# Order of squares, token sums and weight sums around the second norm of a hybrid encoder block

## The chip, the core and the metric

The kernel runs on one core of one Trainium2 chip. The time is device microseconds of one execution; of several runs the median is given. Beside the times there is one profiled execution, whose trace holds every instruction of every engine: TensorE (PE, with its weight loads as PEld), VectorE (DVE), ScalarE (ACT), GpSimd (POOL) and the DMA queues of SyncE (SP), ScalarE and GpSimd.

## The reference

One encoder block over 1024 tokens of width 1024, all in float32. Only the second half of it is touched by the change.

```python
h = rms_norm(x, norm1_g)
proj = h @ w_in                        # q, k, v (8 heads x 64) and u
a = neighbourhood_attention(q, k, v, rpb)
p = multiscale_pool(u, w_pool, pool_scale)
x = x + concat(a, p) @ w_out
h2 = rms_norm(x, norm2_g)              # x * rsqrt(mean(x*x) + 1e-6) * g
x = x + (silu(h2 @ w_gate) * (h2 @ w_up)) @ w_down     # d_ff = 2816
```

## The kernel before

**Number format.** Every operand of a product is split into a high part (a cast to fp32r on ScalarE) and a residue (a subtraction on VectorE), by the helper `split`; the helpers `cook_w` and `split_op` call it for weights and activations. A product is three matmuls: high x high, high x low, low x high. TensorE writes to PSUM banks of 128x512.

**Stages.** Projections and attention come first, up to about 314 us. Then the output product is finished: the residual stream lies transposed in eight tiles `x2[0..7]` of [128, 2, 512], where `x2[0..3]` are the first half of the tokens and `x2[4..7]` the second. Each half tile needs eight blocks `c` of the mixed channels (three matmuls each). For the first half, six of the blocks have been multiplied ahead; `w_full(t, nh, (2, 3), 1)` adds the last pair of blocks, 2 and 3, of which block 3 needs the attention's last values. For the half tiles `t` = 4 and 5 of `nh` = 0, six blocks stand open in PSUM: their generators lie in the list `tail`, and each `next` issues one more block. The other half tiles are done whole (24 matmuls). VectorE adds each finished bank into `x2` (line 818).

**The second norm.** For each token half: ScalarE squares the tiles (`square`, line 948), GpSimd adds the squares into one (line 950), `fold` adds the two halves of that tile on GpSimd (line 956) and splits it, and `tok_sum` lets TensorE sum over the channels with a matrix of ones into the bank `ss`. The last tile of the second half, `x2[7]`, is not added on GpSimd but squared and split in two parts (`square1`, line 960), so the second half has three pairs of token sums. `scale2` makes the reciprocal root (VectorE 968, ScalarE 972 and 973, VectorE 974 to 976), `norm2` scales `x2` in place (VectorE, 984). `store` writes the un-normalised tiles to DRAM through ScalarE's queue.

**Gate and up products.** They are computed from 2x2 block operands with seven products instead of eight, by sums of weights and of activations. A unit `i` is one of 22 (gate and up of 11 column groups). Of each weight, `sum_w` makes the sums s1, s2, s3 (GpSimd, lines 1023 to 1025; for unit 3 VectorE) and `sum_4` the sum s4, in place of block "12" (GpSimd, line 1015), which must wait for the split of "12" and of s2. Activations get sums t1 to t4 (`sub`, line 998). A unit's products are `first` (block 11), `second` (12), `part_y` (s2 x t2), `part_z` (s3 x t3), `part_w` (s1 x t1), `part_4` (22 x t4) and `part_5` (s4 x 22); `add` (line 1063) combines their banks on VectorE, `settle` applies silu (ScalarE, 1068) or multiplies gate and up (line 1072). Units 0 to 3 are interleaved by hand in the order written out below line 1149; from unit 4 on a loop runs, where `sum_4` is called in `cook_w(i, "s4")`. `park` combines a finished pair of units (GpSimd, 1133) and stores it to DRAM with four DMAs from GpSimd's queue (lines 1139 to 1142). The down product reads these tiles back at the end, from about 800 us.

**What sets the order.** Each engine runs its instructions in one fixed order. A scheduler sets that order when the kernel is built, from a model of the times and the order of the program. Instructions passed through `keep` (ScalarE), `keepd` (VectorE), `keepp` (GpSimd) or the matmul helper `mm` keep the order of the program among themselves while the flag `pin_act`, `pin_dve`, `pin_pool` or `pin` is true; all others may be moved. `pin` and `pin_pool` are true from the pairs of blocks 2 and 3 on, `pin_act` and `pin_dve` from just behind `w_full(7, 1)`, all four to just before the loop. Tiles of SBUF come from a ring of 45 buffers of 4 KB a partition (`slot`), so a load can also wait for a buffer to be freed. Loads of weights (`fetch_w`, line 1008) go through SyncE's queue.

Of the kernel before, what the change touches and what calls it, by code (L numbers as in the profile page):

```python
# [42 lines left out]
EARLY = 4  # L43
# [6 lines left out]
def hybrid_block(ctx, tc, xT, xt, w1, wu, rpbx, wpool, wout, wgu, wd, sm, out):  # L50
    nc = tc.nc
# [50 lines left out]
    def keep(i):  # L102
        if pin_act:
            tc.keep_in_program_order(i)
# [5 lines left out]
    def keepp(i):  # L110
        if pin_pool:
            tc.keep_in_program_order(i)
# [374 lines left out]
    pin_act = pin_dve = True  # L487
    for i in range(4):
# [3 lines left out]
        else:  # L492
            g = cook_w1_(0, 0)
# [8 lines left out]
    pin_act = pin_dve = False  # L502
# [17 lines left out]
    pin_act = pin_dve = True  # L520
# [306 lines left out]
    x2 = []  # L827
# [94 lines left out]
    def act_op(o):  # L922
        ACTO[o] = [
            [slot(F32R, f"b{o}_{q}_{nm}", [P, 2, 512]) for nm in "hl"] for q in range(2)
        ]
# [8 lines left out]
    def tok_sum(hf, hl, first, last):  # L934

        if first:
            ps2[hf] = bank(pop, f"ss_{hf}")
        for n in range(2):
            mm(ps2[hf], ones, hl[:, n], start=first and n == 0, stop=last and n == 1)

    def store(hf, q):
        nc.scalar.dma_start(out=x2d[q + 4 * hf], in_=x2[q + 4 * hf])

    acc = {}

    def square(hf, q):
        s = slot(F32, f"sq_{hf}_{q}", [P, 2, 512])
        keep(nc.scalar.activation(s, x2[q + 4 * hf], AF.Square))
        if q:
            keepp(nc.gpsimd.tensor_tensor(out=acc[hf], in0=acc[hf], in1=s, op=ALU.add))  # L950
        else:
            acc[hf] = s
# [10 lines left out]
    def scale2(hf):  # L963
        n = slot(F32, f"n2_{hf}", [P, 2, 512])
        n2[hf] = y = slot(F32, f"y2_{hf}", [P, 512])
        v, a = n[:, 0], n[:, 1]
        keepd(
            nc.vector.tensor_scalar(
                out=v, in0=ps2[hf], scalar1=1.0 / DM, scalar2=EPS, op0=ALU.mult, op1=ALU.add
            )  # L970
        )
        keep(nc.scalar.activation(a, v, AF.Ln))
        keep(nc.scalar.activation(y, a, AF.Exp, scale=-0.5))
        keepd(nc.vector.tensor_tensor(out=a, in0=y, in1=y, op=ALU.mult))
        keepd(nc.vector.scalar_tensor_tensor(out=a, in0=a, scalar=-0.5, in1=v, op0=ALU.mult, op1=ALU.mult))
        keepd(nc.vector.scalar_tensor_tensor(out=y, in0=a, scalar=1.5, in1=y, op0=ALU.add, op1=ALU.mult))

    def norm2(hf, *qs):
        for q in qs:
            x = x2[q + 4 * hf]  # L980
            for i in range(2):
                k = 2 * q + i
                keepd(
                    nc.vector.scalar_tensor_tensor(
                        out=x[:, i],
                        in0=x[:, i],
                        scalar=g2_sb[:, k : k + 1],
                        in1=n2[hf],
                        op0=ALU.mult,
                        op1=ALU.mult,  # L990
                    )
                )

    def split_op(o, q, src):
        split(*ACTO[o][q], src)

    def sub(out, a, b_):
        keepd(nc.vector.tensor_tensor(out=out, in0=a, in1=b_, op=ALU.subtract))
# [4 lines left out]
    def fetch_w(i):  # L1003
        m, f = MF[i]
        raww[i] = []
        for j in range(2):
            r = slot(F32, f"raw_{'gu'[m]}_{f}_{j}", [P, 2, 512])
            nc.sync.dma_start(out=r, in_=wgu[m, f, j])
            raww[i].append(r)
        (r0, r1) = raww[i]  # L1010
        sums[i] = {"11": r0[:, 0], "12": r1[:, 0], "22": r1[:, 1], "s3": r0[:, 1], "s4": r1[:, 0]}

    def sum_4(i):
        x = sums[i]["12"]
        keepp(nc.gpsimd.tensor_tensor(out=x, in0=x, in1=sums[i]["s2"], op=ALU.subtract))
# [12 lines left out]
    def cook_w(i, o):  # L1028
        if i < EARLY and o in ("11", "12"):
            w = rg.tile([P, 2, 512], F32R, tag="w", name=f"w_{i}_{o}")  # L1030
        else:
            w = slot(F32R, f"w_{i}_{o}", [P, 2, 512])
        wop[i, o] = w
        if o == "s4" and i >= EARLY:
            sum_4(i)
        split(w[:, 0], w[:, 1], sums[i][o])

# [46 lines left out]
    def part_y(i, y, hook=None):  # L1084
        u2 = res[i][0][:, 1]
        ps = bank(y, f"y_{i}")
        product(i, ps, "s2", "t2", False)
        if hook:
            hook("s2")
        add(u2, ps, u2)  # L1090
# [38 lines left out]
    def park(i):  # L1129
        f = MF[i][1]  # L1130
        a, b_ = res[i]
        sa, sb = res[i - 1]
        tt = lambda **k: keepp(nc.gpsimd.tensor_tensor(**k))  # L1133
        tt(out=sa[:, 0], in0=a[:, 1], in1=b_[:, 1], op=ALU.add)
        tt(out=sa[:, 1], in0=sa[:, 0], in1=a[:, 0], op=ALU.subtract)
        tt(out=sb[:, 0], in0=a[:, 0], in1=a[:, 1], op=ALU.subtract)
        tt(out=sb[:, 1], in0=b_[:, 0], in1=sa[:, 1], op=ALU.subtract)
        d = gsd[f].rearrange("o p n -> p o n")
        nc.gpsimd.dma_start(out=d[:, 0:1], in_=a[:, 0:1])
        nc.gpsimd.dma_start(out=d[:, 1:3], in_=b_)  # L1140
        nc.gpsimd.dma_start(out=d[:, 3:5], in_=sa)
        nc.gpsimd.dma_start(out=d[:, 5:7], in_=sb)
        del res[i], res[i - 1]

    def w_full(t, nh, cs=eight, n=2):
        for _ in w_out(t, nh, cs, n):
            pass

    pin = pin_pool = True
    for nh in range(2):  # L1150
        for t in range(4):
            w_full(t, nh, (2, 3), 1)
            if t % 2:
                store(0, 2 * nh + t // 2)
                square(0, 2 * nh + t // 2)
# [12 lines left out]
    square(1, 0)  # L1168
    w_full(6, 0)
    tok_sum(0, hl, True, True)  # L1170
    scale2(0)
    for q in range(4):
        norm2(0, q)
        split_op("11" if q < 2 else "21", q % 2, x2[q])
    w_full(7, 0)
    store(1, 1)
    square(1, 1)
    fetch_w(2)
    cook_w(2, "11")
    cook_w(2, "12")  # L1180
    sum_w(2)
    for i in range(2):
        sum_4(i)
    for t in (4, 5):
        w_full(t, 1)
    store(1, 2)
    square(1, 2)
    hl = [fold(1)]
    sum_4(2)
    s67 = slot(F32, "sq_1_3", [P, 2, 512])  # L1190
    w_full(6, 1)
    hl.append(square1(s67, 0))
    w_full(7, 1)
    pin_act = pin_dve = True
    hl.append(square1(s67, 1))
    store(1, 3)
    tok_sum(1, hl[0], True, False)
    tok_sum(1, hl[1], False, False)
    xs = [bank(stp, f"x_{i}") for i in range(EARLY)]
    first(0, xs[0])  # L1200
    tok_sum(1, hl[2], False, True)
    scale2(1)
    first(1, xs[1])
    fetch_w(3)
# [23 lines left out]
    settle(2, 0, 0, xs[2])  # L1228
    settle(3, 0, 0, xs[3])
    part_y(0, mmp)  # L1230
    act_op("t3")
    sub(x2[4], x2[6], x2[4])
    split_op("t3", 0, x2[4])
    sum_w(3, nc.vector, keepd)
    sum_4(3)
    cook_w(3, "s2")
    part_y(1, mmp)
    sub(x2[5], x2[7], x2[5])
    part_y(2, mmp)
    cook_w(0, "s3")  # L1240
# [43 lines left out]
    park(1)  # L1284
    part_4(2)
    cook_w(4, "12")
    cook_w(3, "s4")
    part_5(2)
    cook_w(4, "s2")
# [262 lines left out]
```

## Time and profile before

| | us |
|---|---|
| median of 3 runs (1018.28 to 1020.58) | 1018.47 |
| profiled execution | 1017.6 |
| its span, first to last instruction | 1015.2 |
| TensorE busy in the span | 992.9 (98%) |
| VectorE busy | 673.7 (66%) |
| ScalarE busy | 415.5 (41%) |
| GpSimd busy | 386.4 (38%) |

The granted TensorE clock is 0.993 of full speed on average. A busy TensorE is one with a matmul in flight, so its 98% includes matmuls that run at a lower clock. In a line of the timeline stand the start, the duration, engine, line of the kernel, operation, output and inputs by the program's names, and in square brackets how long the engine was idle before and what ended that. A line of the chain has start, duration and what. A duration on VectorE or GpSimd includes the time for which the instruction is held once it has begun.

### The profile page before, as it was taken

How to read it: one execution, taken by the hardware profiler on the slowest of the kernel's cores; microseconds unless marked ns; L12 is line 12 of the kernel's file. 1: busy time of each engine (PE TensorE's matmuls, PEld its weight loads, DVE VectorE, ACT ScalarE, POOL GpSimd, SP SyncE). 2: the span in 40 equal slices, each digit the busy share in tenths (PEclk: the TensorE clock that was granted, in tenths of full speed). 3: DMA queues.
4: the chain of work that ended last, by engine and by line, in shares of the span. 5: the costliest groups of instructions: out<-in, count | busy, mean ns of one | idle time of the engine just before them, and what ended most of it. 6: DMA issues, size and time to landing. Idle time of an engine off the chain costs nothing.

```text
span 1015.2 us, 13245 instructions
## 1 busy us (share of the span) xinstructions
PE 992.9 (98%) x4801; PEld 843.0 (83%) x4801; DVE 673.7 (66%) x1076; ACT 415.5 (41%) x796; POOL 386.4 (38%) x424
## 2 busy tenths in 40 slices
PE   9999999999999969998999999999999999999998
PEld 9988989998887857786888888888888888888887
DVE  5778777657843759876865555545561599988872
ACT  7634665656633433433333233233241354432500
POOL 0001433333422551068767757657743400000170
PEclk9999999999999979999999999999999999999999
DMA  9412642347814220124233323323317984373302
GB/s 357 177 57 87 220 135 65 100 134 261 267 42 146 84 83 21 53 93 145 76 121 114 110 88 114 103 94 114 110 57 229 357 287 142 101 235 122 125 32 94
DMA packets 56177, 135.88 MB, mean 134 GB/s; under 512 B 5872, under 2 KB 14832, under 8 KB 56112
## 3 DMA queue, kind: packets, MB, share of 16 engines
q1 hardware_dynamic: 48032, 106.45, 31.6%
q0 software_dynamic: 6784, 24.38, 6.3%
q10 hardware_dynamic: 1296, 4.21, 1.1%
q8 instruction: 38, 0.62, 0.3%
q14 instruction: 27, 0.22, 0.1%
HBM read 98.05 MB, written 32.77 MB: 129 GB/s over the span
## 4 chain that ended last, share of the span: by engine, by line
PE 85%; POOL 5%; DVE 5%; issue 2%; ACT 2%; DMA 0%; ACTq 0%; POOLq 0%; DVEq 0%
PE pj L85 12%; PE x L85 11%; PE w L85 10%; PE z L85 9%; PE pc L85 6%; PE pa L85 6%; PE pd L85 6%; PE pw L85 5%; PE y L85 5%; PE pu L85 4%; PE pb L85 3%; PE po L85 3%; PE s L85 2%; PE pt L90 2%; POOL gr L1133 1%
## 5 line engine op out<-in xcount | busy, mean ns | idle before, releaser
L85 PE MATMUL x<-b_h,w 128*128 128x512 f32 x352 | 115.8, 392 | 0.0
L85 PE MATMUL pw<-mx,wo 128*128 128x512 f32 x384 | 91.1, 392 | 1.4 <-ACT mx L763 0.8
L85 PE MATMUL pj<-w1h,xh 128*128 128x384 f32 x256 | 87.6, 347 | 1.7 <-DVE vnl L302 1.7
L85 PE MATMUL pj<-w1l,xh 128*128 128x384 f32 x256 | 84.8, 335 | 1.1 <-DVE w1l L116 1.1
L85 PEld LDWEIGHTS pw<-mx,wo 128*128 128x128 f32 x384 | 71.0, 188 | 16.7 <-ACT mx L763 1.2
L622 POOL TENSOR_SCALAR e<-e,r 64x128 f32<-64x128 f32 (+2 forms) x96 | 52.8, 564 | 83.1 <-DVE r L617 44.6
L85 PE MATMUL pj<-w1h,xl 128*128 128x384 f32 x256 | 83.8, 336 | 0.0
L1477 POOL TENSOR_TENSOR x2r<-x2r,u 128x512 f32<-128x512 f32 x12 | 23.8, 2018 | 149.8 <-DMA raw_a<-gsd 149.8
L1072 POOL TENSOR_TENSOR ur<-ur,gr 128x512 f32<-128x512 f32 x33 | 51.8, 1572 | 70.0 <-DVE ur L1063 31.4
L85 PEld LDWEIGHTS x<-b_h,w 128*128 128x128 f32 x352 | 66.8, 190 | 14.0
L85 PE MATMUL x<-b_l,w 128*128 128x512 f32 x176 | 68.9, 392 | 0.0
L85 PE MATMUL w<-b_h,w_s 128*128 128x512 f32 x176 | 59.1, 397 | 3.5 <-ACT w_s L115 3.1
L116 DVE TENSOR_TENSOR w_s<-sa,w_s 128x512 fp32r<-128x512 f32 x44 | 45.5, 1037 | 23.9 <-ACT w_s L115 23.8
L115 ACT CAST a_h<-raw_a 128x1024 fp32r<-128x1024 f32 (+1 forms) x42 | 41.0, 978 | 49.3 <-PE pc L85 13.8
L85 PE MATMUL y<-bt_h,w_s 128*128 128x512 f32 x176 | 57.7, 390 | 1.7 <-DVE w_s L116 0.9
L85 PE MATMUL z<-bt_h,w_s 128*128 128x512 f32 x176 | 57.9, 390 | 0.0
L85 PE MATMUL w<-bt_h,w_s 128*128 128x512 f32 x176 | 57.8, 389 | 0.0
L85 PE MATMUL z<-bt_h,w 128*128 128x512 f32 x176 | 57.8, 389 | 0.0
L116 DVE TENSOR_TENSOR a_l<-raw_a,a_h 128x1024 fp32r<-128x1024 f32 (+1 forms) x42 | 49.7, 1187 | 3.4 <-ACT a_h L115 3.1
L85 PEld LDWEIGHTS pj<-w1h,xh 128*128 128x128 f32 x256 | 48.5, 190 | 3.3 <-DVE vnl L302 2.5
L85 PEld LDWEIGHTS pj<-w1l,xh 128*128 128x128 f32 x256 | 48.1, 188 | 1.4 <-DVE w1l L116 1.4
L85 PEld LDWEIGHTS pj<-w1h,xl 128*128 128x128 f32 x256 | 48.1, 188 | 0.0
(267 smaller groups left out, 2646.5 us busy)
## 6 DMA issues: line engine op xcount, KB each, us to landing
raw_a<-gsd SPq DMA_DIRECT2D x77, 256.0 KB, 3.9
raw_g<-in_wgu SPq DMA_DIRECT2D x22, 512.0 KB, 3.8
raw_u<-in_wgu SPq DMA_DIRECT2D x22, 512.0 KB, 4.3
gsd<-gr POOLq DMA_DIRECT2D x22, 512.0 KB, 4.0
raw_d<-in_wd SPq DMA_DIRECT2D x20, 512.0 KB, 4.6
nb<-in_rpbx SPq DMA_DIRECT2D x24, 384.0 KB, 3.9
raw_w<-in_w SPq DMA_DIRECT2D x15, 384.0 KB, 4.5
gsd<-ur POOLq DMA_DIRECT2D x11, 512.0 KB, 3.3
```

The lines of the kernel that those rows point to most:

```text
L85: i = nc.tensor.matmul(*a, **k)
L90: i = nc.tensor.transpose(*a)
L115: keep(nc.scalar.copy(h, src))
L116: keepd(nc.vector.tensor_tensor(out=l, in0=src, in1=h.bitcast(F32), op=ALU.subtract))
L622: nc.gpsimd.tensor_scalar(out=out, in0=in0, scalar1=s1, scalar2=1.0, op0=ALU.mult, op1=ALU.mult)
L1072: k(eng.tensor_tensor(out=res[i][c][:, l], in0=src, in1=g, op=ALU.mult))
L1133: tt = lambda **k: keepp(nc.gpsimd.tensor_tensor(**k))
L1477: nc.gpsimd.tensor_tensor(out=q, in0=q, in1=U2[c], op=ALU.add)
```

## The change

Nothing is computed differently; instructions are put in another order, and more of them are held to it.

- `store` and the four DMAs of `park` are pinned as well.
- For the two open half tiles (`tail`), the block 2 product is issued ahead of the eight last pairs, block 3 behind them as before.
- `pin_act` is true from `scale2(0)` on instead of from behind `w_full(7, 1)`.
- `norm2` and `split_op` of the first half come behind `w_full(7, 0)`, `store(1, 1)`, `square(1, 1)` and `fetch_w(2)` instead of ahead of them.
- `sum_4(1)` moves from ahead of the `w_full(4, 1)` and `sum_4(2)` from ahead of `w_full(6, 1)`, both to behind the last `store`.
- `square(1, 2)` comes ahead of `store(1, 2)`.
- `first(0)` comes ahead of all token sums of the second half.
- `sum_w(3)`, `sum_4(3)` and the split of s2 of unit 3 come ahead of the sums t3.
- `sum_4(4)` is called behind `cook_w(4, "12")`, no longer in `cook_w(4, "s4")`, which stands behind `park(3)`.

```diff
     def store(hf, q):
-        nc.scalar.dma_start(out=x2d[q + 4 * hf], in_=x2[q + 4 * hf])
+        keep(nc.scalar.dma_start(out=x2d[q + 4 * hf], in_=x2[q + 4 * hf]))
...
-        if o == "s4" and i >= EARLY:
+        if o == "s4" and i > EARLY:
             sum_4(i)
...
-        nc.gpsimd.dma_start(out=d[:, 0:1], in_=a[:, 0:1])
-        nc.gpsimd.dma_start(out=d[:, 1:3], in_=b_)
-        nc.gpsimd.dma_start(out=d[:, 3:5], in_=sa)
-        nc.gpsimd.dma_start(out=d[:, 5:7], in_=sb)
+        keepp(nc.gpsimd.dma_start(out=d[:, 0:1], in_=a[:, 0:1]))
+        keepp(nc.gpsimd.dma_start(out=d[:, 1:3], in_=b_))
+        keepp(nc.gpsimd.dma_start(out=d[:, 3:5], in_=sa))
+        keepp(nc.gpsimd.dma_start(out=d[:, 5:7], in_=sb))
...
     pin = pin_pool = True
+    for g in tail:
+        next(g)
     for nh in range(2):
         for t in range(4):
             w_full(t, nh, (2, 3), 1)
...
     tok_sum(0, hl, True, True)
+    pin_act = True
     scale2(0)
-    for q in range(4):
-        norm2(0, q)
-        split_op("11" if q < 2 else "21", q % 2, x2[q])
     w_full(7, 0)
     store(1, 1)
     square(1, 1)
     fetch_w(2)
+    for q in range(4):
+        norm2(0, q)
+        split_op("11" if q < 2 else "21", q % 2, x2[q])
     cook_w(2, "11")
     cook_w(2, "12")
     sum_w(2)
-    for i in range(2):
-        sum_4(i)
+    sum_4(0)
     for t in (4, 5):
         w_full(t, 1)
+    square(1, 2)
     store(1, 2)
-    square(1, 2)
     hl = [fold(1)]
-    sum_4(2)
     s67 = slot(F32, "sq_1_3", [P, 2, 512])
     w_full(6, 1)
     hl.append(square1(s67, 0))
     w_full(7, 1)
-    pin_act = pin_dve = True
+    pin_dve = True
     hl.append(square1(s67, 1))
     store(1, 3)
-    tok_sum(1, hl[0], True, False)
-    tok_sum(1, hl[1], False, False)
+    for i in (1, 2):
+        sum_4(i)
     xs = [bank(stp, f"x_{i}") for i in range(EARLY)]
     first(0, xs[0])
-    tok_sum(1, hl[2], False, True)
+    for i in range(3):
+        tok_sum(1, hl[i], i == 0, i == 2)
     scale2(1)
     first(1, xs[1])
...
     part_y(0, mmp)
-    act_op("t3")
-    sub(x2[4], x2[6], x2[4])
-    split_op("t3", 0, x2[4])
     sum_w(3, nc.vector, keepd)
     sum_4(3)
     cook_w(3, "s2")
+    act_op("t3")
+    sub(x2[4], x2[6], x2[4])
     part_y(1, mmp)
+    split_op("t3", 0, x2[4])
...
     part_4(2)
     cook_w(4, "12")
+    sum_4(4)
     cook_w(3, "s4")
```

## The prediction

> **What bounds the kernel now.** I read the page first, its chain and slices.
>
> ```profile
> PE   9999999999999969998999999999999999999998
> PEclk9999999999999979999999999999999999999999
> ...
> PE 85%; POOL 5%; DVE 5%; issue 2%; ACT 2%; DMA 0%; ACTq 0%; POOLq 0%; DVEq 0%
> ```
>
> TensorE carries the chain; only slices 15 and 19 (355 to 381 us and 457 to 482 us) dip, so the change can gain only where TensorE waits. Next, busy time by stage (us; then busy us and records of PE, PEld, DVE, ACT, POOL; clock; DMA).
>
> ```profile
> 362.30:369.90 7.60, 0.00 (x0) 0.00 (x0) 1.56 (x2) 0.63 (x2) 7.52 (x6) 0.66 0.37 152
> 369.90:376.90 7.00, 6.63 (x19) 4.87 (x20) 2.48 (x3) 2.56 (x5) 0.56 (x1) 0.64 0.00 0
> 376.90:396.10 19.20, 19.20 (x86) 15.93 (x85) 16.96 (x22) 9.35 (x15) 0.62 (x1) 1.00 0.00 0
> 470.05:473.18 3.13, 0.00 (x0) 0.00 (x1) 0.71 (x2) 1.30 (x3) 3.11 (x4) 1.00 0.63 126
> 473.18:478.15 4.97, 4.56 (x13) 3.34 (x14) 4.97 (x4) 3.07 (x6) 3.83 (x3) 0.66 0.84 343
> 490.00:800.00 310.00, 310.00 (x1369) 256.72 (x1368) 169.24 (x206) 97.47 (x161) 188.52 (x148) 1.00 0.36 124
> ```
>
> The last row gives the free pace: 310 / 1369 = 0.227 us a matmul; from 490 us on nothing waits, so later stages only move along. Two stalls matter. **Stall B**: nothing runs from 362.3 to 369.9, then 18 matmuls (12 of `first(0)`, 6 token sums) run at a granted clock of 0.64 until 376.9. At the free pace they take 18 x 0.227 = 4.1 us; of 14.6 us, 10.5 are lost. **Stall D**: idle 3.13 us from 470.05, then 12 matmuls in 4.97 instead of 2.72 us: 5.4 us lost. Two small ones, A (315 us) and C (405 us), come below. The timeline and the chain say what ends B.
>
> ```profile
> 342.60 0.63 ACT L973 ACTIVATE y<-n 128x512 f32<-128x512 f32 x1
> 353.02 1.06 ACT L948 ACTIVATE sq<-x 128x1024 f32<-128x1024 f32 x1
> 354.15 2.40 POOL L950 TENSOR_TENSOR sq<-sq,sq 128x1024 f32<-128x1024 f32 x1 [12.30 <-ACT sq L948]
> 356.56 2.24 POOL sa L1023
> 358.87 2.15 POOL sa L1024
> ...
> 364.38 1.22 POOL raw_u L1015
> ...
> 367.97 1.27 POOL sq L956
> 369.27 0.63 ACT sq_hl_a L115
> 369.94 0.80 PE L85 MATMUL ss<-sq_hl_a,ones 128*128 128x512 f32 x1 [7.67 <-ACT sq_hl_a L115]
> ```
>
> GpSimd idles 12.3 us until `square(1,1)`, which stands on ScalarE behind four casts; then one add of squares, `sum_w(2)` (three), `sum_4(0)`, `sum_4(1)`, the next add of squares and the fold run one behind the other.
>
> **Part by part.**
>
> *Stall B.* `square(1,1)` moves ahead of norm2 and its casts: behind the Exp of `scale2(0)` (343.2) and a store issue (0.33), to 343.6 to 344.7, against 353.0 now. Its add on GpSimd starts near 345 instead of 354.15. `sum_4(1)` (1.22) and `sum_4(2)` leave the queue ahead of the fold. `first(0)` (12 matmuls, 2.7 us) goes ahead of all token sums, so TensorE has work from 362.3 to 365.0. Without a collision, the sums would end at 362.3 + 4.1 = 366.4: 10.5 us earlier. The store pinned behind the square delays nothing: norm2 of that tile stands some 20 us later.
>
> But the earlier GpSimd work now meets norm2 on VectorE, whose cover so far are GpSimd's 12.30 us of idleness.
>
> ```profile
> 346.60 5.38 DVE L984 SCALAR_TENSOR_TENSOR x<-x,sm_sb,y 128x512 f32<-128x512 f32 x8
> 353.03 1.21 DVE L116 TENSOR_TENSOR b_l<-x,b_h 128x1024 fp32r<-128x1024 f32 x1
> 354.17 0.68 DVE L818 TENSOR_TENSOR x<-pw,x 128x512 f32<-128x512 f32 x1
> 354.77 5.10 DVE L116 TENSOR_TENSOR b_l<-x,b_h 128x1024 fp32r<-128x1024 f32 x2
> 129.54 0.16 DVE L99 SCALAR_TENSOR_TENSOR rsq_q<-rsq_q,v 128x8 f32<-128x8 f32 x1
> 250.94 2.74 POOL L622 TENSOR_SCALAR e<-e,r 128x384 f32<-128x384 f32 x6 [6.82 <-DVE r L617]
> 252.14 1.22 DVE L99 SCALAR_TENSOR_TENSOR rsq_q<-rsq_q,v 128x8 f32<-128x8 f32 x1
> ```
>
> With GpSimd at work two `b_l` take 5.10 us where one alone took 1.21, and the sums 2.24 and 2.15 where the 128x512 fold took 1.27: they take turns. The add from PSUM stays at 0.68. Norm2 next to GpSimd is not in the trace. Its bounds: untouched (0.67 us each), or in full turns. The nearest row is L99, the same operation with two SBUF inputs: 0.16 us alone, 1.22 while GpSimd ran. I take turns.
>
> [...]
>
> In turns, from 345.4 (end of the `scale2` arithmetic, for which the load below waits): one add of squares 2.4 + four sums of 1.27 + eight norm2 of 0.67 = 12.9, to 358.3. Two `b_l` (2.4) and the add from PSUM that completes x2[6]: 361.3. `square(1,2)` 1.06, the add of squares 2.4, one `b_l` in between 1.2, the fold 1.27: 367.2. Cast 0.63, two half squares with their casts (four operations some 0.6 apart), the last VectorE residue 0.7, the last matmul: about **371.0**. If the last PSUM add stands behind two weight splits that alternate with `sum_4(1)` and `sum_4(2)`, 1.9 more. So `scale2(1)` and `first(1)` begin 376.9 - 371.0 = 5.9 us earlier; the seven products behind them run without a gap (19.2 us in the row to 396.1), so that shift carries on. TensorE has then idled most of 365 to 371, and after 3.13 us of idleness in stall D the clock fell to 0.66 and 12 matmuls lost 4.56 - 2.72 = 1.8. Today that slow stretch lies ahead of 376.9; then it lies behind. B brings 5.9 - 1.8 = **4.1**, ends 2 and 10.5.
>
> The loads decide too: `sum_w(2)` needs `fetch_w(2)`.
>
> ```profile
> 345.56 0.33 SPq L1008 DMA_DIRECT2D raw_g<-in_wgu  x1
> ...
> SPq L1008 <- DVE y L976: 4.5, 1, 4.5
> ...
> raw_g<-in_wgu SPq DMA_DIRECT2D x2, 512.0 KB, 3.5
> ```
>
> Its second half waits 4.5 us for a buffer that `scale2(0)` frees, then lands 3.5 us later, at 349: inside the 12.9 us counted, so nothing added.
>
> *Stall A, open products ahead.* Six matmuls (two products of block 2) move ahead of the eight last pairs.
>
> ```profile
> 315.42 0.50 PE L85 MATMUL pw<-mx,wo 128*128 128x512 f32 x1 [0.80 <-ACT mx L763]
> 316.15 1.21 PE L85 MATMUL pw<-mx,wo 128*128 128x512 f32 x4 [0.22 <-DVE mx L766]
> 333.24 1.12 DVE L116 TENSOR_TENSOR sq_hl_a<-sq,sq_hl_a 128x512 fp32r<-128x512 f32 x1 [3.33 <-ACT sq_hl_a L115]
> 334.46 0.62 PE L85 MATMUL ss<-sq_hl_a,ones 128*128 128x512 f32 x2
> ```
>
> They fill the 1.0 us wait, but the pairs still start at 316.15, so the first token sum is still ready at 334.36, just when TensorE arrives today (334.46). With six matmuls fewer between (1.4 us), TensorE now waits there. Late next: the fold. I take **0.2** (the first of the two sums goes early); ends -0.3 and 1.0.
>
> *Stall C, `sum_w(3)` ahead of t3.*
>
> ```profile
> 401.78 1.23 DVE L116 TENSOR_TENSOR bt_l<-x,bt_h 128x1024 fp32r<-128x1024 f32 x1 [1.12 <-ACT bt_h L115]
> ...
> 406.68 0.73 PE L85 MATMUL y<-bt_h,w_s 128*128 128x512 f32 x2 [0.91 <-DVE w_s L116]
> ...
> 414.22 0.19 PEld L85 LDWEIGHTS w<-bt_l,w_s 128*128 128x128 f32 x1 [0.52 <-DVE bt_l L116]
> ```
>
> The third part y waits for s2 of weight 3, now some 3 us earlier on VectorE: that wait goes. But the t3 splits move back behind it, and the first z needs them; VectorE's list up to the t1 split, for which the first w waits at 414.22, is the same in another order, and so is what is late next. Only a part of VectorE's 1.12 us of idleness can be won: **0.3**, ends -0.5 and 1.7 (0.8 + 0.9, both waits there).
>
> *Stall D, `sum_4(4)` earlier, GpSimd's stores pinned.*
>
> ```profile
> 456.87 0.73 POOL L1142 DMA_DIRECT2D gsd<-gr  x1
> 457.63 2.54 POOL L1072 TENSOR_TENSOR ur<-ur,gr 128x512 f32<-128x512 f32 x2
> 457.85 4.12 DVE L116 TENSOR_TENSOR w<-raw_g,w 128x512 fp32r<-128x512 f32 x1
> 471.20 1.27 POOL L1015 TENSOR_TENSOR raw_g<-raw_g,sa 128x512 f32<-128x512 f32 x1
> 472.51 0.62 ACT L115 CAST w_s<-raw_g 128x512 fp32r<-128x512 f32 x1 [1.07 <-POOL raw_g L1015]
> ```
>
> `sum_4(4)` runs at 471.20, behind the whole of `park(3)`; the cast at 472.51 and TensorE's s4 product wait for it. It moves behind `park(1)`, before the pair at 457.63. The pin also moves one store issue, which today runs in idle GpSimd time, into `park(1)` (0.73): start near 458.4 (457.63 and 0.73), end 459.7, cast 460.3, residue at the worst 4.1 (the row at 457.85): 464.4, where TensorE needs it at 470.05. The wait goes with 5 us to spare, and with it the slow clock: **5.4**, ends 3.1 (the idle alone) and 5.4. Behind it on GpSimd `sum_w(5)` and `park(3)` run some 2 us later; TensorE needs the former only after two more products (5.4 us), so nothing shows. The four issues of `park(3)`, one moved in as well, are read back only in the down stage.
>
> **The sum**, against the profiled execution (1017.6 us, span 1015.2; the median is 1018.47, 0.9 above): 4.1 + 0.2 + 0.3 + 5.4 = 10.0, so **1007.6 us**. By themselves the ends of B that I hold likely (sums 1.5 us earlier or later than 371.0) with C's and A's ends give 1005 to 1010.
>
> **The rivals.**
>
> *No turns: 1002.* Norm2 runs untouched next to GpSimd, or VectorE's list gets its PSUM adds early. Then norm2 ends at 352 as today, x2[6] is squared by 359, the sums end about 367.5, and TensorE hardly idles, so the clock stays: B = 9.4; 1017.6 - 9.4 - 5.4 - 0.5 = 1002.3. For it: the PSUM adds keep 0.68 next to GpSimd. Against: L99 and the `b_l` row. [...]
>
> *Stall D stays or its place is taken: 1012.* GpSimd runs without a gap from 457.6 to 475; with TensorE arriving 3 us earlier something else behind `sum_4(4)`, the i=5 sums first, may be late. Then D brings 0.5 to 2 of its 5.4: 1010 to 1013. Against: the 5 us to spare.
>
> *Nothing to measure: 1017.* The waits reappear in full: VectorE starts `scale2(1)` near 376, D stays. 1014.5 to 1020.7. Pinned order on three engines speaks against it.
>
> *Slower: 1024.* The buffer. `sq_1_1` is taken ten microseconds earlier, and buffers are short: the second load of `fetch_w(2)` waits 4.5 us already. If it must wait for one freed at the end of the output products (362.3) or later, `sum_w(2)`, pinned on GpSimd ahead of the squares, holds them up: load 3.5, three sums and `sum_4(0)` 5.1, squares 2.4, fold 1.3, cast and halves 3.6 give sums at 378.2 already. From a landing near 371.6 on, sums at 384, the loss (7.1, and 1.8 to the clock) outweighs A, C and D (5.9) by the 3 that can be measured. Landing at 375: 387.4, a loss of 12.3 - 5.9, about 1024. Against: the buffer freed by `scale2(0)` is freed as before, and loads now stand ahead of the `b` tiles in the program.
>
> **How the numbers follow.** About 0.3% (3.05 us) is what a measurement of this kernel can tell from no change. Forecast with turns (1005 to 1010) 0.50; no turns (1001 to 1005) 0.24; D not won (1010 to 1014) 0.13; nothing 0.08; slower 0.05. Faster: the first three, 0.87; same 0.08; slower 0.05. The range 1001.5 to 1013.5 takes in the first three but their edges, some 0.83. Its ends: 1001.5 is B without any collision (10.5), D in full and 0.2 of A and C; 1013.5 is B at 2, D at 2, the rest at nothing.
>
> **What would show it.** B: the second half's first add of squares on GpSimd near 345, norm2 rows stretched beyond 0.67 and the rows of `sum_w(2)` beyond 1.27; token sums after `first(0)`, the last near 371, a granted clock below 1 there. Norm2 at 5.4 in all and sums at 367 would show the first rival. A: no wait at 315, one of about 1 us before the first half's token sums. C: no wait in y, one in the first z. D: `sum_4(4)` near 458 in today's times, no idle ahead of the first s4 product there, clock 1.00. Wrong I am above all if VectorE's order of adds, which no pin fixes until 362, differs from today's, or if a load comes late.

## The result and the profile after

| | before | after |
|---|---|---|
| median of the comparison runs | 1018.38 us (4 runs) | 1009.33 us (4 runs) |
| lowest to highest | 1017.36 to 1020.58 | 1009.10 to 1009.74 |
| profiled execution, span | 1017.6, 1015.2 | 1009.33, 1007.0 |

The ratio after to before is 0.9909, with a 95% interval of 0.9892 to 0.9926: 9 us faster. The forecast was 1007.6 us with a range of 1001.5 to 1013.5.

The first view is the page of the changed kernel: the forty slices (25.2 us each) of TensorE and of its granted clock, and the chain's shares.

```profile
PE   9999999999999989999999999999999999999998
...
PEclk9999999999999989999999999999999999999999
...
PE 85%; DVE 6%; POOL 5%; issue 2%; ACT 1%; DMA 1%; DVEq 0%; POOLq 0%; ACTq 0%
```

The slice that held stall D (457 to 482 us) is at 9 tenths like its neighbours; the one with stall B is up from 6 to 8 tenths, and its clock from 7 to 8. The next view is busy time by stage (us; then busy us and records of PE, PEld, DVE, ACT, POOL; clock; DMA).

```profile
361.00:373.10 12.10, 8.71 (x29) 5.99 (x29) 7.80 (x10) 4.39 (x7) 8.72 (x4) 0.79 0.52 173
373.10:393.00 19.90, 19.90 (x85) 16.35 (x85) 17.85 (x23) 9.97 (x15) 0.00 (x0) 0.96 0.00 0
440.00:470.00 30.00, 30.00 (x134) 24.85 (x133) 25.28 (x22) 9.93 (x18) 29.70 (x22) 1.00 0.39 132
470.00:560.00 90.00, 89.47 (x394) 73.46 (x394) 62.35 (x66) 29.86 (x53) 66.39 (x54) 1.00 0.34 120
```

Up to the end of the second half's token sums TensorE now idles 3.4 us (12.10 - 8.71), where the rows of before gave 7.6 and 0.4, and it idles not at all from 440 to 470. A new idleness of 0.53 us appears between 470 and 560. Where it waits, the timeline of TensorE says (start, length, ..., in brackets the idle time ahead and what ended it):

```profile
335.51 0.49 PE L85 MATMUL ss<-sq_hl_a,ones 128*128 128x512 f32 x1 [1.99 <-DVE sq_hl_a L116]
...
368.55 0.79 PE L85 MATMUL ss<-sq_hl_a,ones 128*128 128x512 f32 x1 [2.58 <-ACT sq_hl_a L115]
...
371.37 1.65 PE L85 MATMUL ss<-sq_hl_s,ones 128*128 128x512 f32 x3 [0.47 <-DVE sq_hl_s L116]
...
405.93 0.74 PE L85 MATMUL z<-bt_h,w_s 128*128 128x512 f32 x2 [1.62 <-DVE w_s L116]
```

Stall A has moved from 315 us to the first half's second token sum and has grown from 1.0 to 1.99 us. Stall C has moved from y to the first z. On VectorE, in the same profile:

```profile
333.07 0.69 DVE L818 TENSOR_TENSOR x<-pw,x 128x512 f32<-128x512 f32 x1 [4.75 <-PE pw L85]
333.68 1.78 DVE L116 TENSOR_TENSOR sq_hl_a<-sq,sq_hl_a 128x512 fp32r<-128x512 f32 x1
...
348.99 8.93 DVE L984 SCALAR_TENSOR_TENSOR x<-x,sm_sb,y 128x512 f32<-128x512 f32 x8
...
457.64 2.36 DVE L116 TENSOR_TENSOR w_s<-raw_g,w_s 128x512 fp32r<-128x512 f32 x1 [1.42 <-ACT w_s L115]
```

and on GpSimd:

```profile
345.24 2.67 POOL L950 TENSOR_TENSOR sq<-sq,sq 128x1024 f32<-128x1024 f32 x1 [3.55 <-ACT sq L948]
347.99 1.63 POOL L1023 TENSOR_TENSOR sa<-raw_g,raw_g 128x512 f32<-128x512 f32 x1
349.69 1.62 POOL L1024 TENSOR_TENSOR sa<-sa,raw_g 128x512 f32<-128x512 f32 x1
...
361.96 4.54 POOL L950 TENSOR_TENSOR sq<-sq,sq 128x1024 f32<-128x1024 f32 x1 [7.25 <-ACT sq L948]
```

Norm2 takes 8.93 us for eight instead of 5.38, and the four sums of GpSimd beside it 1.62 to 1.75 us each, where the fold alone took 1.27: the two take turns. The output product's last add now stands ahead of the fold's residue on VectorE, in the other order than before.

**Landmarks.** All kernels below are compared by four starts in their own profiles, counted from the start of the residue of mx (VectorE, line 766), since what lies ahead of it is the same code: "scale 1" and "scale 2" are the first VectorE operation of `scale2` for each half (line 968), "first y" the first matmul of `part_y(0)`, "down" the first matmul of the down stage. From "down" to the end each takes 213.3 us (e9 213.6). Each row of the table is one execution, and a granted clock that fell in one and not in the other can move a landmark by some 1.6 us (last section).

| kernel | scale 1 | scale 2 | first y | down | median us |
|---|---|---|---|---|---|
| before | 25.76 | 61.68 | 80.52 | 486.45 | 1017.6 to 1018.4 |
| after | 26.93 | 57.85 | 77.61 | 478.47 | 1009.33 |
| e1, no open products | 25.72 | 56.64 | 76.18 | 477.07 | 1008.63 |
| e2, sum_4(4) late | 28.44 | 59.35 | 79.17 | 487.68 | 1019.54 (one) |
| e3, factor in PSUM | 28.54 | 55.39 | 74.25 | 475.15 | 1005.83 |
| e4, sums of unit 2 late | 26.92 | 54.88 | 74.05 | 475.12 | 1007.57 |
| e5, sum_4(4) alone | 25.76 | 61.85 | 80.69 | 489.97 | 1021.13 |
| e8, e3 and e1 | 25.75 | 52.61 | 71.47 | 472.27 | 1003.11 |
| e9, all stores free | 28.50 | 59.41 | 79.30 | 488.02 | 1019.20 |
| e10, order kept | 26.58 | 57.52 | 77.61 | 478.45 | 1009.95 |
| e13, park(1) pinned | 28.49 | 59.39 | 79.17 | 484.48 | 1014.57 |
| e14, park(3) pinned | 26.95 | 57.86 | 77.78 | 482.38 | 1013.74 |
| e15, t3 first | 26.91 | 57.81 | 77.74 | 479.17 | 1013.14 (one) |
| e16, part D alone | 25.71 | 62.50 | 81.36 | 483.35 | 1013.37 |

Read for before and after, the change costs 1.17 us up to scale 1 (part A), brings 4.08 from there to the first y (54.76 to 50.68: part B) and 5.07 from there to the down stage (405.93 to 400.86: parts C and D). Together 7.98; the span fell by 8.2.

### The profile page after: what moved, and what is told of

Its sections match the earlier page's. It is cut to its first block, busy times and chain, and to the rows that moved or that the text cites. A ratio compares the mean times of both kernels' runs of the same rounds, so it can differ in the third digit from the quotient of the medians.

```text
span 1007.0 us, 13239 instructions
## 1 busy us (share of the span) xinstructions
PE 991.2 (98%) x4801; PEld 841.9 (84%) x4801; DVE 685.3 (68%) x1076; ACT 414.7 (41%) x796; POOL 391.9 (39%) x424
## 4 chain that ended last, share of the span: by engine, by line
PE 85%; DVE 6%; POOL 5%; issue 2%; ACT 1%; DMA 1%; DVEq 0%; POOLq 0%; ACTq 0%
PE pj L85 12%; PE x L85 10%; PE w L85 10%; PE z L85 10%; PE pw L85 6%; PE pc L85 6%; PE pa L85 6%; PE pd L85 6%; PE y L85 4%; PE pu L85 4%; PE pb L85 3%; PE po L85 3%; PE s L85 2%; PE pt L90 1%; POOL gr L1133 1%
## 5 line engine op out<-in xcount | busy, mean ns | idle before, releaser
L116 DVE TENSOR_TENSOR w_s<-sa,w_s 128x512 fp32r<-128x512 f32 x44 | 53.1, 1209 | 21.9 <-ACT w_s L115 21.7
```

The costliest lines, as they stand in the source:

```text
L116: keepd(nc.vector.tensor_tensor(out=l, in0=src, in1=h.bitcast(F32), op=ALU.subtract))
```

## The experiments

Each is the changed kernel with one edit, if nothing else is said.

### e1: no open products ahead (part A undone)

```diff
-    for g in tail:
-        next(g)
     for nh in range(2):
```

> The changed kernel without the two open block 2 products ahead of the last pairs. Theory (the first half's token sums set the end, the open products only move the wait, and with them one PSUM add slips ahead of the fold's residue): TensorE waits 1.0 us at 315 us again, the first half's sums end near 335.0 instead of 336.0, the second half's about 0.9 us earlier, and the time falls to about 1008.4 us. Rival (the products ahead save the wait at 315 us): about 1 us longer, 1010.3 us. Second rival (the second half's chain is set elsewhere): sums of the first half earlier, second half and time unchanged at 1009.3 us.

Measured: 1008.63 us (1007.78 to 1010.03), ratio 0.9914, 0.9897 to 0.9930. TensorE's timeline in this run:

```profile
316.10 0.49 PE L85 MATMUL pw<-mx,wo 128*128 128x512 f32 x1 [0.80 <-ACT mx L763]
316.83 18.43 PE L85 MATMUL pw<-mx,wo 128*128 128x512 f32 x80 [0.23 <-DVE mx L766]
335.10 0.62 PE L85 MATMUL ss<-sq_hl_a,ones 128*128 128x512 f32 x2
```

The two small waits are back and the one of 1.99 us is gone; scale 1 is 1.21 us earlier than in the changed kernel, the down stage 1.40. So part A costs 1.2 to 1.4 us by the landmarks; the medians (0.7 apart, intervals overlapping) cannot confirm it by themselves.

### e10: the open products kept, the old order on VectorE kept too

```diff
-        nc.vector.tensor_tensor(out=x, in0=ps, in1=x, op=ALU.add)
+        keepd(nc.vector.tensor_tensor(out=x, in0=ps, in1=x, op=ALU.add))
...
+    pin_dve = True
     hl = fold(0)
+    pin_dve = False
...
+    pin_dve = True
     w_full(6, 0)
+    pin_dve = False
```

> The changed kernel with the open products kept, and two instructions more kept in program order on VectorE: the residue of the first half's fold and, behind it, the PSUM add of the output product 6 of the first half, which the changed kernel runs the other way round. Theory: stall A turned from +0.2 into a loss of about 1.1 us because of this order: with the fold first, TensorE's wait ahead of the second token sum falls from 1.99 to about 0.9 us, the first half's sums end 25.7 us behind the residue of mx (26.93 in the changed kernel), down stage near 477.3 instead of 478.47, time 1.2 lower: 1008. Rival: the residue is late since GpSimd's fold is (1.78 us for a residue that took 1.12 is GpSimd's work beside it): wait 1.7 or more, time unchanged.

Measured: 1009.95 us (1009.26 to 1010.53), ratio 0.9919, 0.9902 to 0.9936. TensorE and then VectorE:

```profile
334.54 0.50 PE L85 MATMUL ss<-sq_hl_a,ones 128*128 128x512 f32 x1 [0.64 <-DVE sq_hl_a L116]
```

```profile
333.37 1.11 DVE L116 TENSOR_TENSOR sq_hl_a<-sq,sq_hl_a 128x512 fp32r<-128x512 f32 x1 [4.68 <-ACT sq_hl_a L115]
...
340.55 0.69 DVE L818 TENSOR_TENSOR x<-pw,x 128x512 f32<-128x512 f32 x1 [2.66 <-PE pw L85]
341.16 1.04 DVE L116 TENSOR_TENSOR w<-raw_u,w 128x512 fp32r<-128x512 f32 x1
342.12 0.68 DVE L968 TENSOR_SCALAR n<-ss 128x512 f32<-128x512 f32 x1
```

Both theories are half right. The flipped order did make the wait: with the fold first, the residue is back to 1.11 us and the wait falls from 1.99 to 0.64. But nothing comes through: scale 1 does not wait for the token sums, it stands on VectorE behind the add of the next output product, some 24 matmuls later, and with this edit the scheduler put a residue (1.04 us) between the two. The 0.35 us that scale 1 still gains is lost within `scale2`: VectorE's last step of it begins at 346.60, behind a PSUM add at 345.99 (345.69 in the changed kernel). First y is at 77.61 in both. What part A costs is thus the time that TensorE idles plus what VectorE's list makes of it, and the wait by itself isn't the price.

### e3: one operand of norm2 in PSUM

The factor of the first half is written to its PSUM bank, and norm2 reads it there; the order of all engines stays.

```diff
+        if hf == 0:
+            n2[hf] = ps2[hf]
-        keepd(nc.vector.scalar_tensor_tensor(out=y, in0=a, scalar=1.5, in1=y, op0=ALU.add, op1=ALU.mult))
+        keepd(nc.vector.scalar_tensor_tensor(out=n2[hf], in0=a, scalar=1.5, in1=y, op0=ALU.add, op1=ALU.mult))
...
-                        in0=x[:, i],
+                        in0=n2[hf],
...
-                        in1=n2[hf],
+                        in1=x[:, i],
```

> The changed kernel with the factor of norm2 of the first half written to the PSUM bank of its token sums, so that those eight norm2 have one SBUF input instead of two; all engines keep their order. Theory (a VectorE instruction with two SBUF inputs and GpSimd take turns): the eight take about 5.4 us instead of 8.9, the four GpSimd sums beside them 1.27 us each instead of 1.62 to 1.75, the second half's token sums end near 369.5 instead of 373.0, and the time is about 1005.5 us. Rival (GpSimd slows any VectorE instruction that reads SBUF): norm2 stays at 8.9 us and the time at 1009.3. Second rival (norm2 gets faster, but GpSimd's or ScalarE's chain sets the sums): norm2 5.4, sums still near 373, time 1009.

Measured: 1005.83 us (1004.11 to 1006.63), ratio 0.9883, 0.9868 to 0.9897. Norm2 on VectorE, then the sums of unit 2 on GpSimd:

```profile
349.93 5.34 DVE L986 SCALAR_TENSOR_TENSOR x<-ss,sm_sb,x 128x512 f32<-128x512 f32 x8
```

```profile
349.50 1.30 POOL L1025 TENSOR_TENSOR sa<-raw_g,raw_g 128x512 f32<-128x512 f32 x1 [0.64 <-DVE ss L978]
350.87 1.30 POOL L1026 TENSOR_TENSOR sa<-sa,raw_g 128x512 f32<-128x512 f32 x1
352.12 1.30 POOL L1027 TENSOR_TENSOR raw_g<-raw_g 128x512 f32<-128x512 f32 x1
```

Beside the same GpSimd work, norm2 takes 5.34 us in place of 8.93 and the sums 1.30 in place of 1.62 to 1.75. The theory of turns is shown for norm2: with its second operand in SBUF, it and GpSimd's sums hold each other up; with that operand in PSUM they do not. From scale 1 to the first y this brings 4.97 us; 1.6 are lost ahead of scale 1 in this profile, to the clock (last section).

### e4: the sums of unit 2 behind the fold

```diff
-    sum_w(2)
-    sum_4(0)
     for t in (4, 5):
         w_full(t, 1)
...
     hl = [fold(1)]
+    sum_w(2)
+    sum_4(0)
```

> The changed kernel with sum_w(2) and sum_4(0) put behind the second fold on GpSimd, so that GpSimd has only the add of squares beside norm2. Theory (turns between norm2 and those sums cost the second half's chain): norm2 about 5.5 to 6.5 us, token sums end at 369 to 370, where the moved sums may hold the last residues by up to 1.3 us, time 1005.5 to 1006.5. Rival (the order of the PSUM adds on VectorE and of ScalarE sets it): sums stay within 1 us of 373, time 1008.5 to 1009.5. Second rival: sum_w(2) now late for the y products of unit 2: a wait in y near 398, time above 1009.

Measured: 1007.57 us (1007.09 to 1009.35), ratio 0.9905, 0.9890 to 0.9920; the down stage is 3.35 us earlier than in the changed kernel. On VectorE:

```profile
350.19 5.37 DVE L984 SCALAR_TENSOR_TENSOR x<-x,sm_sb,y 128x512 f32<-128x512 f32 x8
...
369.28 1.43 DVE L116 TENSOR_TENSOR sq_hl_s<-sq,sq_hl_s 128x512 fp32r<-128x512 f32 x1 [0.26 <-ACT sq_hl_s L115]
```

The same from the other side: with GpSimd idle beside it, norm2 is back at 5.37 us with both operands in SBUF. The moved sums then hold up the last residues a little (1.17 and 1.43 us, where the two took 2.20 together in the changed kernel). The medians show 1.8 us of the landmarks' 3.35, and the time is above the expected 1005.5 to 1006.5.

### e8: the factor in PSUM and no open products

Both edits, e3 and e1, together.

> The changed kernel with the first half's norm factor in PSUM and without the two open products of block 2 ahead of the last pairs (stall A left as before). Theory: the two edits act in different places and add up: norm2 5.3 us in all, the first half's sums about 25.7 us behind the residue of mx (changed kernel 26.93, factor in PSUM alone 28.54 because TensorE's clock fell behind its wait of 1.99 us), down stage at 475.15 - 2.8 = 472.4, time about 1003.0 (1005.8 for the factor alone). Rival: the second half's chain hangs on GpSimd's queue, which starts with the loads and not with the first half's sums; then only part comes through: 1004.5 to 1005.5.

Measured: 1003.11 us (1002.63 to 1003.68), ratio 0.9851, 0.9837 to 0.9866, against the expected 1003.0; the down stage at 472.27 against 472.4. The two add up, and this kernel is faster than both: what is left of stall B is one wait of about 1 us (0.97), and the granted clock of the profiled execution is 1.00 on average.

```profile
366.63 1.10 PE L85 MATMUL ss<-sq_hl_s,ones 128*128 128x512 f32 x3 [0.97 <-DVE sq_hl_s L116]
```

### e15: t3 ahead of sum_w(3) (part C undone)

```diff
+    act_op("t3")
+    sub(x2[4], x2[6], x2[4])
+    split_op("t3", 0, x2[4])
     sum_w(3, nc.vector, keepd)
     sum_4(3)
     cook_w(3, "s2")
-    act_op("t3")
-    sub(x2[4], x2[6], x2[4])
     part_y(1, mmp)
-    split_op("t3", 0, x2[4])
```

> The changed kernel with the difference and the split of t3 put back ahead of sum_w(3), the order of before. Theory: part C is worth 0.6 us as the landmarks gave it (0.3 was predicted): two waits come back in y (0.8 and 0.9 us), the wait of 1.62 us in the first z goes, and the third w starts 0.5 to 0.7 us later relative to the first y; everything behind moves along, down stage 479.1 us behind the residue of mx (478.47). Rival: what C won is lost again behind it, where GpSimd's run from 455 to 486 us decides: down stage unchanged.

Measured, in one run: 1013.14 us, of which 3 us lie ahead of the residue of mx, so it is read by the landmarks alone. TensorE's waits:

```profile
405.10 0.50 PE L85 MATMUL y<-bt_h,w_s 128*128 128x512 f32 x1 [0.80 <-ACT w_s L115]
...
406.74 0.73 PE L85 MATMUL y<-bt_h,w_s 128*128 128x512 f32 x2 [0.91 <-DVE w_s L116]
```

Both waits in y are back, the one in z is gone, and the down stage is 0.70 us later (479.17), 0.57 of it behind the first y. Part C is worth 0.6.

### e2: sum_4(4) late (one half of part D undone)

```diff
-        if o == "s4" and i > EARLY:
+        if o == "s4" and i >= EARLY:
...
-    sum_4(4)
     cook_w(3, "s4")
```

> The changed kernel with sum_4(4) back in the split of s4 of unit 4, so behind park(3), and nothing else undone. Theory (that move alone removes stall D, 5.5 us by the positions of the s4 product, of which about 1.05 us is given back by 505 us): an idle time of some 3 us ahead of the s4 product of unit 4, a clock near 0.66 behind it, and 1013.8 to 1014.9 us. Rival (the earlier start of the whole second norm or the pinned stores account for it): within 1 us of 1009.3.

Measured, in one run: 1019.54 us, some 5 more than expected. TensorE:

```profile
474.52 0.80 PE L85 MATMUL w<-b_h,w_s 128*128 128x512 f32 x1 [5.41 <-ACT w_s L115]
```

Stall D is back, and larger than before the change (3.13 us idle). From the first y to the down stage the move costs 7.65 us (408.51 against 400.86); another 1.5 lie ahead of scale 1 and come from the clock (last section). 7.65 was more than stall D had held, and asked for the next runs.

### e5: sum_4(4) early and nothing else

The kernel before with the same move of sum_4(4), its stores not pinned.

> The kernel before with one edit: sum_4(4) behind cook_w(4, '12') as after the change; the stores of park stay unpinned, everything around the second norm as before. The run with sum_4(4) put back in the changed kernel was 9.2 us later at the down stage (487.68 against 478.47 us behind the residue of mx), more than the 5.4 that stall D of the kernel before held. Theory: D alone is worth its stall, 5.4: about 1012.4 us, down stage 481.0 us behind the residue of mx (before: 486.45), no idle ahead of the s4 product of unit 4; the rest of the 9.2 is a stall that the other parts would have made longer (an earlier TensorE and four pinned store issues on GpSimd). Rival: D is worth 9 by itself: 1009. Rival: without the pinned stores the early sum is no use, below 2 us: 1016 or more.

Measured: 1021.13 us (1020.46 to 1021.84), ratio 1.0030, 1.0019 to 1.0041: slower than before, where 1012.4 was expected. Only the third theory is left, and it said too little: without the pinned stores the early sum doesn't just fail to help, it costs 3.4 us from the first y to the down stage (409.28 against 405.93).

### e9: the stores of park free

```diff
-        keepp(nc.gpsimd.dma_start(out=d[:, 0:1], in_=a[:, 0:1]))
+        nc.gpsimd.dma_start(out=d[:, 0:1], in_=a[:, 0:1])
```

and so for all four.

> The changed kernel with the four stores of park not kept in program order on GpSimd, as before the change. Theory: the pinned issues (0.7 us each, eight of them between 452 and 480 us) lengthen GpSimd's gapless stretch from 455 to 486 us, and are the cause of the 1.05 us that the changed kernel gives back between 469 and 505 us: 1008.3, down stage 477.4 us behind the residue of mx. Rival: the issues take GpSimd's time wherever they stand, and the loss there comes from its sums: no change, 1009.3 and 478.5.

Measured: 1019.20 us (1017.76 to 1020.14), ratio 1.0015, 1.0005 to 1.0024. Freeing the stores costs 9.9 us by the medians, where a gain of 1 or no change was expected; 7.9 of it lie between the first y and the down stage (408.72 against 400.86), 1.6 ahead of scale 1. Both theories fall. Nearly all of the loss hangs on one row; VectorE first, then GpSimd beside it, then TensorE:

```profile
461.91 10.07 DVE L116 TENSOR_TENSOR w_s<-raw_g,w_s 128x512 fp32r<-128x512 f32 x1
471.90 0.68 DVE L1063 TENSOR_TENSOR gr<-z,gr 128x512 f32<-128x512 f32 x1
```

```profile
460.77 0.75 POOL L1140 DMA_DIRECT2D gsd<-ur  x1
461.55 1.31 POOL L1024 TENSOR_TENSOR sa<-sa,raw_u 128x512 f32<-128x512 f32 x1
462.80 1.30 POOL L1025 TENSOR_TENSOR raw_u<-raw_u 128x512 f32<-128x512 f32 x1
464.05 1.29 POOL L1133 TENSOR_TENSOR gr<-ur,ur 128x512 f32<-128x512 f32 x1
...
470.18 1.25 POOL L1025 TENSOR_TENSOR raw_g<-raw_g 128x512 f32<-128x512 f32 x1
476.96 1.68 POOL L1015 TENSOR_TENSOR raw_u<-raw_u,sa 128x512 f32<-128x512 f32 x1 [5.53 <-DVE w L116]
```

```profile
472.73 0.77 PE L85 MATMUL z<-bt_h,w 128*128 128x512 f32 x1 [7.22 <-DVE gr L1063]
```

The residue starts 0.36 us behind the start of a GpSimd operation and then stands through eight of them; it ends at 471.98, just behind the end of GpSimd's run (470.18 + 1.25 = 471.43). GpSimd's operations keep their undisturbed 1.25 to 1.31 us: no turns here. Behind the residue the adds from PSUM wait, and TensorE needs the banks. In the changed kernel the same residue, at 457.64, takes 2.36. Run e5 has the same rows 1.9 us later: 463.79, 10.08 us, and 7.22 of waiting. A store issue stands right ahead of that run of GpSimd operations; in the changed kernel the pin holds it back to the end of `park`.

### e13 and e14: the stores of one pair pinned

```diff
+        pk = keepp if i == 1 else (lambda s: s)
-        keepp(nc.gpsimd.dma_start(out=d[:, 0:1], in_=a[:, 0:1]))
+        pk(nc.gpsimd.dma_start(out=d[:, 0:1], in_=a[:, 0:1]))
```

and so for all four; e14 has `i == 3`.

> The changed kernel with only the stores of park(1) kept in program order on GpSimd; those of park(3) are free, so one of them (the store of b_) slips in between the sums of unit 5, as in the run with all stores free, where the residue of sum_4(4) stood 10.07 us on VectorE behind it and the kernel lost 9.5 us at the down stage (488.02 against 478.47 us behind the residue of mx). Theory 1, the slipped issue: VectorE is kept out when its residue arrives beside the first GpSimd operation after a store issue, until GpSimd's run of operations ends; that happens here: a residue of about 10 us, TensorE idle about 7 us, 1017 to 1019. Theory 2, the pause: what counts are the four issues in a row at 453 to 456 us, in which VectorE gets the residue ahead of sum_4(4) done; they are all here, so 1008.5 to 1009.5 and no residue over 2.5 us between 455 and 475.

> The mirror: only the stores of park(3) kept in program order, those of park(1) free, so two of its four issues leave the pause at 453 to 456 us and none slips in between the sums of unit 5. Theory 1, the slipped issue: no residue of 10 us near 462; the one that stood 5.36 us from 456 in the run with all stores free, behind the last issue of park(1), may stay, but TensorE has 5 us in hand there: 1008 to 1011. Theory 2, the pause: without it the residue of sum_4(4) is late as in that run: 1017 to 1019.

Measured: e13 1014.57 us (1013.06 to 1016.62), ratio 0.9971, 0.9959 to 0.9982; e14 1013.74 us (1012.98 to 1014.58), ratio 0.9965, 0.9952 to 0.9978. VectorE and GpSimd in e13:

```profile
464.43 10.76 DVE L116 TENSOR_TENSOR w<-raw_u,w 128x512 fp32r<-128x512 f32 x1
```

```profile
463.91 0.75 POOL L1141 DMA_DIRECT2D gsd<-ur  x1
464.68 1.30 POOL L1024 TENSOR_TENSOR sa<-sa,raw_u 128x512 f32<-128x512 f32 x1
```

and VectorE and TensorE's waits (waiter, what it waited for, total, times, longest) in e14:

```profile
495.85 7.10 DVE L116 TENSOR_TENSOR w<-raw_u,w 128x512 fp32r<-128x512 f32 x1
```

```profile
PE z L85 <- DVE gr L1063: 3.0, 1, 3.0
```

The pause theory is out: e13 has the pause and a residue of 10.76 us; e14 has only two of its four issues left, and its s4 product of unit 4 is on time. The slipped issue fits all these runs: with it the long residue is there, without it that one isn't. How an issue brings this about isn't shown. The times that went with the theory were both off. From the first y to the down stage e13 loses 4.45 us and e14 3.74 against the changed kernel. In e13 the residue caught was another one, which TensorE needs later (2.85 us of idleness, not 7); in e14 a second long residue came up 35 us later, again at a store issue (GpSimd's at 495.33), and cost 3 us.

Over all 14 profiles, from 440 to 620 us, there are 1030 residues of 128x512. 26 of them stand longer than 3 us, and 25 of these began during a store issue on GpSimd or within 0.6 us of the start of the first operation behind one. Of the 509 that began during any other GpSimd operation, one did (3.61 us). A store issue is thus nearly always there, yet not enough: some 170 residues began at such a place. What else decides was not found.

### e16: both halves of part D, nothing else

The kernel before with sum_4(4) early and the stores of park pinned.

> The kernel before with both halves of part D and nothing else: sum_4(4) behind cook_w(4, '12') and the stores of park kept in program order on GpSimd. Each half without the other lost (1021.1 us for the early sum alone, 1019.5 for the pin with A, B and C). Theory: together they remove stall D of the kernel before, 5.4 us, less the 1.05 that the changed kernel gives back behind it: down stage 481.0 to 482.1 us behind the residue of mx (before: 486.45), time 1012.4 to 1013.5, no residue over 4 us on VectorE between 455 and 475. Rival: D is worth 9 also in the kernel before, since the pin removes long residues there too: 477.5, 1009. Rival: the fit of residues and GpSimd operations is a matter of where they happen to meet, and here a residue of 7 us or more stands somewhere between 455 and 510: 1015 or more.

Measured: 1013.37 us (1012.24 to 1014.13), ratio 0.9952, 0.9935 to 0.9968. From the first y to the down stage 401.99 us against 405.93: 3.94 us, as the first theory had it (5.4 less 1.05 is 4.35). No residue over 4.0 us. So the two halves only work together: from the first y to the down stage the early sum alone costs 3.4 us (e5), the pin alone 2.6 (e2, with C's gain in it), and both together bring 3.9.

## Why the prediction was right, and where not

**Stall B: right in mechanism; that the size fits is partly luck.** Predicted 4.1, measured 4.08. Turns between norm2 and GpSimd, the step that decided between the forecast and the faster rival, were shown by e3 and e4; norm2 ended at 357.9 (predicted 358.3), x2[6] was complete at 360.8 (361.3). But scale 1 began 1.0 us later than the prediction had it (342.14 instead of 341.16, stall A), so the turns themselves took some 1.4 us less than its 12.9. The second add of squares met a `b_l` and two weight residues and took 4.54 us where the prediction had 3.6 (2.4, and 1.2 for one `b_l`), and from the fold's end (367.8) to the last token sum (373.0) it took 5.2 instead of 3.8. So the sums ended 2.0 later than the 371.0 predicted, 1.0 of it stall A: counted from scale 1 they came 4.9 us earlier and not 5.9. The slow clock behind them was put at 1.8; the clock of 0.96 over 19.9 us is 0.8. These two misses of 1.0 cancelled.

**Stall A: wrong, in sign.** Predicted +0.2 with ends of -0.3 and 1.0; it cost 1.2, and 1.6 more in profiles where the clock fell behind its wait (last section). The step that failed is "TensorE now waits there", with a wait of about 1 us, and "Late next: the fold". The fold came when predicted, but the add of output product 6 stood ahead of its residue on VectorE (the danger named last in the prediction), and the residue met GpSimd's sum and took 1.78 instead of 1.12. Run e10 adds a second fault in that step: it took the token sums for what releases `scale2`, and that stands behind the next output product's add.

**Stall C: right, with the size too small.** The wait went from y to the first z as predicted, 0.6 instead of 0.3.

**Stall D: right in its result, wrong in a step.** The wait and the slow clock went, 5.4 us, as predicted. But the step "residue at the worst 4.1 (the row at 457.85)" is no bound: residues of 10.07 and 10.76 us stand in e9 and e13. And the pin was counted as a cost of 0.73 us; in truth it is what the gain hangs on, 7.9 us. Had the sum been moved without it, the rival "its place is taken" would have come true, and worse than its 1012. The prediction was right there partly by luck.

**Not foreseen: 1.05 us given back behind D.** The step that failed is "so nothing shows". Between the end of the s4 product of unit 4 and the down stage the changed kernel takes 324.59 us, the kernel before 323.54. Of this, 0.8 is one wait with the restart behind it, a row of this answer of the waits of TensorE (455 to 520 us, changed kernel):

```profile
PE z L85 <- DVE gr L1063: 0.5, 1, 0.5
```

Another 0.2 is at the s4 product of unit 5, whose weight load stood for VectorE, too briefly to show as idleness of TensorE:

```profile
486.26 0.19 PEld L85 LDWEIGHTS w<-b_h,w_s 128*128 128x128 f32 x1 [0.37 <-DVE ur L1063]
```

Everywhere else in between matmul follows matmul every 0.227 us. Both delays are there in e16 too and neither is there before the change, so they belong to D.

The sum: -1.17 + 4.08 + 0.57 + 5.4 - 1.05 = 7.8, of 8.2 in the span, against 10.0 predicted. The slower rival didn't happen: the second load of `fetch_w(2)` came early enough.

## What to carry to other kernels

Before GpSimd work is moved beside VectorE work, count the VectorE operations with two SBUF operands. With one operand of norm2 in PSUM the two passed each other here (5.34 us for eight instead of 8.93), and that was worth 3.5 us by the medians, nearly the 4.1 of the whole reordering of the norm. A store issued from GpSimd's queue in the midst of its sums could cost far more here than its own 0.75 us (TensorE waited 7.22 us in e9), though most such issues had no long row beside them: hold them to the end of the run, and look for single VectorE rows many times their usual length. And two edits that each lose can win together, so an edit that looks like housekeeping (a pin on four stores) has to be undone by itself before it is called free.

## What was not expected of the hardware

**Standing through a run.** Beside the sums, norm2 lost 0.44 us an operation ((8.93 - 5.38) / 8), less than the length of one sum (1.62 to 1.75); in e9 a row of 10.07 us stood through eight operations of 1.3. 18 of the 26 long residues end 0.55 us behind the end of GpSimd's gapless run, so they stood through all that was left of it. The mirror is in the changed kernel: GpSimd's add of squares at 361.96 (4.54 us, undisturbed 2.40) ends 2.25 us behind the last of three VectorE residues in a row (364.26). When the two take turns, as norm2 and the sums do, and when one stands through the other's run, is not shown by any run here.

**The same wait, two clocks.** The wait of 1.99 us ahead of the first half's second token sum stands in eight profiles. In four of them TensorE's clock fell behind it, in four it stayed at 1.00. The window from 337 to 341 us, in the changed kernel and in e2 (clock is the third number from the end):

```profile
337.00:341.00 4.00, 4.00 (x19) 3.31 (x18) 3.55 (x3) 0.00 (x0) 3.92 (x3) 1.00 0.82 258
```

```profile
337.00:341.00 4.00, 4.00 (x12) 3.14 (x12) 4.00 (x3) 0.19 (x1) 3.92 (x3) 0.62 0.46 144
```

Those whose clock fell reach scale 1 at 28.4 to 28.5 us instead of 26.9, so such a wait costs 1.6 us more in some executions than in others. The clock records of the traces show what goes with it, but for one case. In each of the 14, all changes of the clock lie whole multiples of 3.41 us apart (in the kernel before they stand at 364.75, 374.99, 473.97 and 477.39 us between 310 and 800), and a low stretch is at 0.50 for one, two or three of these windows. The cases differ in how much of a wait falls into one window. Two neighbouring windows of e13, then of e4:

```profile
333.31:336.72 3.41, 1.56 (x6) 0.75 (x4) 2.31 (x2) 3.02 (x6) 3.33 (x4) 1.00 0.01 2
336.72:340.13 3.41, 3.27 (x8) 2.60 (x9) 3.41 (x4) 0.64 (x1) 3.33 (x3) 0.50 0.42 130
```

```profile
334.95:338.36 3.41, 1.60 (x7) 1.37 (x8) 3.41 (x4) 2.31 (x4) 3.41 (x3) 1.00 0.10 13
338.36:341.77 3.41, 3.41 (x17) 2.83 (x16) 3.41 (x3) 0.00 (x0) 3.33 (x3) 1.00 0.83 264
```

In e13 TensorE idles 1.85 us of the window and the next one has half the clock; in e4 it idles 1.81 us, the rest of the same wait lies in the window ahead, and the clock stays. From 310 to 800 us in all traces, each of the 21 windows at full clock with 1.85 us of idleness or more has one at 0.50 behind it; of those with 1.81 or less one has (1.70 us, in e16). Where a wait falls among the windows differs from execution to execution, so part of each landmark is luck. Here 1.85 us of idleness in a window of 3.41 was thus enough; in the changed kernel one idle for 1.95 us (364.51 to 367.92) has half the clock behind it, one idle for 1.73 (333.79 to 337.20) has not.
